# One-core decoder block: a third late MoE unit, x2 added on VectorE, g_final by a transfer, the overflow loop's body written once

## The chip, the cores and the metric

The kernel runs on one core of a Trainium2 chip. The metric is the device time of one launch in microseconds, the median of several runs. TensorE is called PE (its weight loads PEld), VectorE DVE, ScalarE ACT, GpSimd POOL and SyncE SP.

## What is computed

A decoder block on x of 256 tokens by 1024, in float32. A mixer (attention and a gated delta rule) gives x2 = x + mixer. Then comes an expert layer with 32 experts, of which each token takes two, a gate that is computed from the result, and a final norm:

```
def hierarchical_moe(h, ...):                 # gate: top-1 group, top-2 expert
    for e in range(N_EXPERTS):
        hid = jax.nn.silu(t @ w_gate[e]) * (t @ w_up[e])
        out = out + gate[:, e:e + 1] * (hid @ w_down[e])
...
        x = x + hierarchical_moe(rmsnorm(x, g_ffn[i]), ...)
        ple_gate = jax.nn.sigmoid(rmsnorm(x, g_ple[i]) @ w_ple_gate[i])
        x = x + ple_gate * (p[i] @ w_ple_proj[i])
    return rmsnorm(x, g_final)
```

A matrix of one expert (`w_gate`, `w_up` or `w_down`) has 1 MB, `w_ple_gate` 4 MB. x3 is the x behind the expert layer.

## The kernel before

**Units.** The experts are sorted by their load and served in nine units: unit 0 of four experts, units 1 and 2 of two, units 3 to 8 of four. A unit's tokens are gathered by a one-hot matmul into `XT`. Then come `gate(i)` and `up(i)` (64 matmuls of 128x32 weights by 256 columns for a unit of four), `hidden(i)` (the product, its transposes to `hidT`), and the down projection in two halves of 512 columns (`dn`). The weights come as 1-MB matrices into a ring of SBUF buffers (names ra, rq, rb, rc, rs), by indirect transfers that POOL issues in order, each as soon as its buffer is free.

**Early units.** What an early unit computes is spread back to the tokens (`parts`, line 1700): ACT copies the half to `yH`, DVE makes `yL`, the rest, and PE adds both by the one-hot `C` into four PSUM banks `total[t][n]` (tile names `sum00` to `sum11`). x2 itself lies as two parts, `xH` and `xL` (`xx0`, `xx1`), which also feed the gathers. `add_x2` (line 1359) adds it to `total` with eight identity matmuls. After the last early unit `early_features` (line 1899) copies each quarter of `total` to `x3` in the PLE buffer `ple[2]`, and transposes it into the features, a tile that `room` (line 1875) places where `xx0` was.

**Late units.** `UE` is the first late unit, `UL` = 8 the last. Before, units 7 and 8 are late. `z_early` (line 1917) makes the gate's product z = features by `w_ple_gate` from the early part of x3, with 32 float32 matmuls of 512 columns into the four `sum` banks, after `gate(UE)`; it needs `w_ple_gate` in four ring buffers, each scaled by g_ple (`scaled`). The tuple `WPG` says ahead of which unit's which matrices this weight is fetched. A late unit's half goes by `late_parts` and `late_spread` into x3 by DVE adds, its transposed form by `z_late` through the same weight (eight pairs of 64-row matmuls for each half), and by `z_spread` (four matmuls with `C2`, which `rows2` makes) into z. Down weights of units from `UE`-1 on come in halves, so that a first half can start earlier (`FIRST`).

**The overflow branch.** A late expert has 16 or 32 slots; tokens beyond a unit's slots are served by `overflow` (line 1720), a loop over the experts under a condition that is false in this run. The body has four windows of 64 tokens, written out four times (`for win in range(T // 64)`), with 78 matmuls in each. `crowded` (line 1796) puts this branch in, in the middle of unit 4.

**g_final** is read by SP as one row of 4 KB, and spread over the partitions by two matmuls with one row of weights and two ACT copies (`ple_rows`, line 1817).

**Order.** Each piece of work is a generator whose `yield after(...)` names what must have been told. A planner (`Plan`) runs them with a cost model and so fixes the order of instructions on each engine at build time; `turn()` passes the one bank `ga` from user to user. All operations pass through one helper, so that nearly every row of the trace has line 77; tiles tell them apart.

Of the kernel before, what the change touches and what calls it, by code (L numbers as in the profile page):

```python
# [6 lines left out]
F32 = mybir.dt.float32  # L7
# [17 lines left out]
UNITS = [[0, 1, 2, 3], [4, 5], [6, 7]] + [list(range(e, e + 4)) for e in range(8, E, 4)]  # L25
NU = len(UNITS)

WPG = (7, "g")

UE, UL = NU - 2, NU - 1  # L30

FEW = 16
FIRST = UNITS[UE - 1][0]
# [258 lines left out]
def hybrid_block(tc, x, p_t, w_in, w_o_fox, w_o_delta, w_out, w_gate, w_up, w_down, w_ple_gate,  # L292
# [1064 lines left out]
    total = [[None, None], [None, None]]  # L1357

    def add_x2():
        S.copy(identr, ident)  # L1360
        G.memset(late_slots, -1.0)
        G.tensor_copy(late_slots[:, 0:FEW], K("slots")[:, 0:FEW])
        yield after("cb", 4 * 4)
        for t in range(2):
            for n in range(2):
                for part in (xH, xL):
                    P.matmul(total[t][n], identr, part[:, t, :, n * 64:(n + 1) * 64].rearrange("p k q -> p q k"),
                             start=False, stop=False)
                yield
        tell("x2in")  # L1370

    def weights():
# [248 lines left out]
    def rows2(i):  # L1621

        yield after("crowd")
        yield after("rows", i + 1)
        yield after("wt", UE // 2 + 1)
        yield after("lp", 4 * max(0, i - UE - 1))
        yield lambda: None if using else 0.0
        using.append(i)
        g = K("w_rt")[:, 0:256].rearrange("p (t c) -> p t c", t=2)
        for t in range(2):  # L1630
            V.tensor_tensor(g[:, t].rearrange("p (a o s) -> p a o s", a=2, o=4),
                            K("slots")[:, None, None, 0:FEW].to_broadcast([128, 2, 4, FEW]),
                            rkp[:, t, None, UNITS[i][0]:UNITS[i][-1] + 1, None].to_broadcast([128, 2, 4, FEW]), op=OP.is_equal)
        yield
        yield turn()
        pc = ps_t("ga")[:, 0:256]
        for t in range(2):
            P.transpose(pc[:, t * 128:(t + 1) * 128], g[:, t], ident)
        using.pop()
        yield  # L1640

        PR["C2", i] = QD[UE // 2][0].rearrange("p t a s -> p (t a s)")[:, i % 2 * 256:i % 2 * 256 + 256]
        S.copy(PR["C2", i], pc)
        tell("ga")
        tell("C2")
        yield
# [4 lines left out]
    def hidden(i, pg):  # L1651
# [20 lines left out]
        S.copy(hT.rearrange("p k s -> p (k s)"), pt)  # L1672
        tell("hT")
        tell("ga")
        names = [f"d{e}" for e in u]
        yield (ring.there(*names) if u[0] < FIRST else ring.arrived((0, 2), *names))
        w = [ring.get(n).rearrange("p (q k d) -> p q k d", q=4, k=2) for n in names]
# [42 lines left out]
    def overflow():  # L1720
# [12 lines left out]
        with tc.If(n > 0):  # L1733
            V.memset(big[:, 0:1], 1.0)
            V.tensor_copy(rg[:, :, 1:2], gr[:, :, 0, 0:1])
            with tc.For_i(0, E) as e:
# [3 lines left out]
                for i, src in ((0, rko), (2, gr[:, :, :, 1])):  # L1740
                    V.tensor_tensor(prod, src, oh, op=OP.mult)
                    V.tensor_reduce(rg[:, :, i:i + 1], prod, axis=AX.X, op=OP.add)
                for win in range(T // 64):
                    for t in range(2):
                        V.tensor_scalar(g[:, t * 64:(t + 1) * 64], K("slots"), float(64 * win), rg[:, t, 0:1],
                                        op0=OP.add, op1=OP.is_equal)
                    for k in range(8):
                        pt = ps_t("ga")
                        m = 0
# [45 lines left out]

    def crowded():
        yield after("flag")
        yield after("x2in")
        ring.cap -= 2
        yield lambda: ring.free[1][2] if len(ring.free) > 1 else None  # L1800
        yield turn()
        ring.cap += 2
        was = dict(plan.free)
        slots = overflow()
        plan.free.update({key: max(was[k] for k in "PSVG") + 4.0 for key in "PSVG"})
        plan.free["D"], plan.end = was["D"], plan.free["P"]
        for slot in slots:
            ring.give(slot)
        tell("ga")
        tell("crowd")  # L1810
        yield
# [5 lines left out]
    def ple_rows():  # L1817
# [5 lines left out]
            ple.append(ring.take(F32)[0])  # L1823
        pT = ple[1][:, 0:512].rearrange("p (k t) -> p k t", k=2)
        nc.sync.dma_start(pT, p_t.rearrange("(k p) t -> p k t", p=128))
        gf = ple[1][:, 1024:2048]
        nc.sync.dma_start(gf[0:1, :], bass.AP(tensor=g_final.tensor, offset=g_final.offset, ap=[[0, 1], [1, D]]))
        at = plan.load(plan.end, 1 << 18)
        yield after("group", 3)
        yield ring.there("wpp0")  # L1830
# [11 lines left out]
                yield  # L1842
        ring.done("wpp0")
        tell("pp")

        for n in range(2):
            yield turn()
            ps = ps_t("ga")
            P.matmul(ps, ones[0:1, :], gf[0:1, n * 512:(n + 1) * 512], start=True, stop=True)
            yield  # L1850
            S.copy(gf[:, n * 512:(n + 1) * 512], ps)
            tell("ga")
            yield

# [17 lines left out]

    def room():

        yield after("crowd")
        yield after("group", (NU + 1) // 2)
        features.append(mr.tile([128, 2, 8, 128], F32, name="xx0"))
        ring.add(mr, "xx", 1, 2)  # L1880
        yield

    features = []
# [15 lines left out]
    def early_features(t):  # L1899

        yield lambda: 0.0 if len(ple) > 2 and features else None
        for n in range(2):
            yield after(f"done{t}", n + 1)
            x = x3(t)[:, n * 512:(n + 1) * 512]
            (V.tensor_copy if n else S.copy)(x, total[t][n])
            yield
            yield turn()
            pt = ps_t("ga")
            for kk in range(4):
                P.transpose(pt[:, kk * 128:(kk + 1) * 128], x[:, kk * 128:(kk + 1) * 128], ident)  # L1910
            yield
            (S.copy if n else V.tensor_copy)(feat(t)[:, 4 * n:4 * n + 4, :].rearrange("p k q -> p (k q)"), pt)
            tell("ga")
            tell(f"a{t}")
            yield
# [345 lines left out]
```

## Time and profile before

| | |
|---|---|
| median of 3 runs | 523.71 us (522.18 to 524.1) |
| the profiled execution | 521.74 us, its span 519.9 us |
| PE busy | 476.1 us (92%) |
| DVE busy | 223.2 us (43%) |
| ACT busy | 202.3 us (39%) |
| mean granted PE clock | 0.969 |
| moved by DMA | 141.23 MB, mean 272 GB/s |

Of the profiled time 1.84 us lie outside the span. The page gives shares over the whole span, and stages differ: the experts run from about 250 us on, and the branch of `crowded` comes at 336 us. What waits there is read from the waits of PE, the chain of waits that ended last, and the stretches of a few microseconds in which the busy time, the granted clock and the DMA share are given.

### The profile page before, as it was taken

The numbers are of one execution on the slowest core, as the hardware profiler recorded it, in microseconds if no ns is written. First come the engines' busy times: TensorE is split into PE (matmuls) and PEld (weight loads), VectorE is DVE, ScalarE is ACT, GpSimd is POOL, SyncE is SP. The second block draws the span as 40 slices with busy tenths as digits, with TensorE's granted clock in tenths as the row PEclk, the third lists the DMA queues.
The fourth block names the chain that finished last, engine by engine and source line by source line (L and its number), as shares of the span: only waits on it lengthen the run. The fifth ranks groups of instructions, "written<-read, shape, count | busy, mean of one in ns | idle before, by whom it ended". The sixth has DMA issues, their size and how long they took to land. (4 is left out here: it accounts for less than half of the span.)

```text
span 519.9 us, 10333 instructions
## 1 busy us (share of the span) xinstructions
PE 476.1 (92%) x4313; PEld 343.1 (66%) x4313; DVE 223.2 (43%) x532; ACT 202.3 (39%) x465; POOL 127.7 (25%) x153
## 2 busy tenths in 40 slices
PE   7999999999999999998999988867868779989993
PEld 7999998889999999877565544434325444334341
DVE  3888779773646748677232111100011140101146
ACT  5675855657654554424322122121210350100244
POOL 5000461300000000033224443412374363260000
PEclk9999999999999999997999999978989799999998
DMA  8944442222279658986499999999999999960002
GB/s 339 366 166 161 162 167 84 84 83 85 79 296 400 238 200 337 421 319 219 156 422 422 420 421 420 414 418 419 418 348 417 420 412 420 387 242 3 1 0 81
DMA packets 25028, 141.23 MB, mean 272 GB/s; under 512 B 2561, under 2 KB 2833, under 8 KB 11538
## 3 DMA queue, kind: packets, MB, share of 16 engines
q0 software_dynamic: 13744, 82.86, 39.2%
q1 hardware_dynamic: 11090, 57.15, 29.1%
q8 instruction: 35, 0.57, 0.5%
q10 hardware_dynamic: 144, 0.52, 0.3%
q14 instruction: 15, 0.12, 0.1%
HBM read 139.46 MB, written 1.05 MB: 270 GB/s over the span
## 5 line engine op out<-in xcount | busy, mean ns | idle before, releaser
L77 PE MATMUL mm<-hH,ra 128*128 128x256 f32 x624 | 116.4, 285 | 0.0
L77 PEld LDWEIGHTS mm<-hH,ra 128*128 128x128 f32 x624 | 96.1, 189 | 1.5 <-issue 0.3
L77 PE MATMUL mm<-hL,ra 128*128 128x256 f32 x312 | 76.4, 282 | 0.5 <-DVE hL L77 0.5
L77 PEld LDWEIGHTS mm<-hL,ra 128*128 128x128 f32 x312 | 58.8, 189 | 1.4 <-DVE hL L77 0.7
L77 DVE TENSOR_TENSOR ra<-ra,ra 128x1024 fp32r<-128x1024 f32 x39 | 48.1, 1237 | 16.5 <-ACT ra L77 16.4
L77 ACT CAST ra<-ra 128x1024 fp32r<-128x1024 f32 x39 | 40.8, 1053 | 24.0 <-PE mm L77 22.0
L77 PE MATMUL dn<-ra,hidT 128*32 128x512 f32 (+2 forms) x108 | 33.5, 624 | 3.4 <-issue 3.1
L77 POOL CAST xx<-xt 128x1024 fp32r<-128x1024 f32 (+1 forms) x2 | 3.3, 1650 | 126.2 <-ACT td L77 123.6
L77 DVE TENSOR_TENSOR yL<-dn,yH 128x512 fp32r<-128x512 f32 x15 | 10.4, 690 | 53.8 <-ACT yH L77 43.5
L77 PE MATMUL up<-ra,XT 128*32 128x256 f32 (+1 forms) x224 | 30.2, 382 | 0.0
L77 ACT ACTIVATE XT<-ga,kp 128x256 f32<-128x256 f32 (+1 forms) x32 | 12.3, 445 | 38.0 <-PE ga L77 31.8
L77 DVE SCALAR_TENSOR_TENSOR kp<-th,wt,up 128x256 f32<-128x256 f32 x9 | 4.3, 480 | 51.4 <-PE up L77 51.4
L77 PE MATMUL gate<-rq,XT 128*32 128x256 f32 (+1 forms) x176 | 24.6, 383 | 1.7 <-issue 1.6
L77 PE MATMUL up<-rb,XT 128*32 128x256 f32 x144 | 23.9, 381 | 0.5 <-issue 0.3
L77 PE MATMUL gate<-ra,XT 128*32 128x256 f32 (+1 forms) x176 | 24.2, 402 | 0.0
L77 PEld LDWEIGHTS ga<-G,xx 128*128 128x128 f32 x128 | 18.5, 215 | 7.9 <-issue 3.7
L77 PE MATMUL ga<-G,xx 128*128 128x256 f32 (+1 forms) x128 | 20.8, 313 | 2.9 <-ACT XT L77 1.5
L77 ACT CAST yH<-dn 128x512 fp32r<-128x512 f32 x15 | 8.8, 587 | 32.8 <-PE sum L77 19.6
L77 PE MATMUL gate<-rb,XT 128*32 128x256 f32 (+1 forms) x112 | 21.0, 416 | 0.3 <-issue 0.3
L77 PE MATMUL dn<-rb,hidT 128*32 128x512 f32 (+1 forms) x64 | 19.1, 612 | 1.0 <-DVE yL L77 1.0
L77 PEld LDWEIGHTS up<-ra,XT 128*32 128x32 f32 (+1 forms) x224 | 14.7, 115 | 7.7 <-issue 2.3
L77 PE MATMUL dn<-rq,hidT 128*32 128x512 f32 (+1 forms) x40 | 19.5, 753 | 0.3 <-DVE yL L77 0.3
(503 smaller groups left out, 1083.8 us busy)
## 6 DMA issues: line engine op xcount, KB each, us to landing
ra<-in_w_in SPq DMA_DIRECT2D x19, 1024.0 KB, 5.4
ra<-in_w_gate SPq DMA_DIRECT2D x4, 1024.0 KB, 4.8
ra<-in_w_out SPq DMA_DIRECT2D x3, 1024.0 KB
ra<-in_w_down SPq DMA_DIRECT2D x3, 1024.0 KB, 11.3
ra<-in_w_o_fox SPq DMA_DIRECT2D x2, 1024.0 KB, 5.7
rq<-in_w_in SPq DMA_DIRECT2D x2, 1024.0 KB, 11.5
rb<-in_w_up SPq DMA_DIRECT2D x2, 1024.0 KB
rb<-in_w_down SPq DMA_DIRECT2D x2, 1024.0 KB, 15.1
```

Source lines behind the costliest of these rows:

```text
L77: return f(*a, **k)
```

## The change

Five things change.

1. `UE` goes from 7 to 6: units 6, 7 and 8 are late, and x3's early part holds six units, 0 to 5. `WPG` moves with it: the gate weight is fetched ahead of unit 6's gate matrices, and unit 5's down weights come in halves too. `z_early` follows `gate(6)`.
2. `add_x2` makes no matmuls. Two DVE instructions for the two token tiles write xH + xL into `x3`, and `early_features` adds each quarter of `total` to it with a DVE add, where it was a copy by ACT or DVE. `crowded` waits for the fourth early part and no longer for x2.
3. The features lie in a ring buffer that `room` takes once unit 4 is in `total`, and both `xx0` and `xx1` go to the ring once the branch and x2 are through.
4. g_final comes by one transfer with its row read for all 128 partitions (512 KB), issued from ACT's queue in `hidden(8)`. The 4-KB transfer on SP, two matmuls and two ACT copies are gone.
5. The overflow body stands once in a loop (`tc.For_i`), with one more DVE instruction that moves the window on.

```
-WPG = (7, "g")
-
-UE, UL = NU - 2, NU - 1
+WPG = (6, "g")
+
+UE, UL = NU - 3, NU - 1
...
     def add_x2():
...
-        yield after("cb", 4 * 4)
+        yield lambda: 0.0 if len(ple) > 2 else None
         for t in range(2):
-            for n in range(2):
-                for part in (xH, xL):
-                    P.matmul(total[t][n], identr, part[:, t, :, n * 64:(n + 1) * 64].rearrange("p k q -> p q k"),
-                             start=False, stop=False)
-                yield
+            V.tensor_tensor(x3(t).rearrange("p (q k) -> p q k", k=8), xH[:, t].bitcast(F32).rearrange("p k q -> p q k"),
+                            xL[:, t].bitcast(F32).rearrange("p k q -> p q k"), op=OP.add)
+            yield
         tell("x2in")
...
-        yield after("rows", i + 1)
+        yield after("rows", max(i + 1, UE // 2 * 2 + 2))
...
+        if i == UL:
+
+            nc.scalar.dma_start(ple[1][:, 1024:2048], bass.AP(tensor=g_final.tensor, offset=g_final.offset, ap=[[0, 128], [1, D]]))
...
-                for win in range(T // 64):
+                with tc.For_i(0, T // 64):
...
+                    V.tensor_scalar(rg[:, :, 0:1], rg[:, :, 0:1], -64.0, None, op0=OP.add)
...
         yield after("flag")
-        yield after("x2in")
+        yield after("cb", 4 * 4)
         ring.cap -= 2
...
-        gf = ple[1][:, 1024:2048]
-        nc.sync.dma_start(gf[0:1, :], bass.AP(tensor=g_final.tensor, offset=g_final.offset, ap=[[0, 1], [1, D]]))
...
-        for n in range(2):
-            yield turn()
-            ps = ps_t("ga")
-            P.matmul(ps, ones[0:1, :], gf[0:1, n * 512:(n + 1) * 512], start=True, stop=True)
-            yield
-            S.copy(gf[:, n * 512:(n + 1) * 512], ps)
...
     def room():
 
+        yield after("cb", 4 * (UE - 1))
+        ring.cap -= 1
+        yield lambda: ring.free[0][2] if ring.free else None
+        features.append(ring.take(F32)[0].rearrange("p (t k q) -> p t k q", t=2, k=8))
         yield after("crowd")
+        yield after("x2in")
         yield after("group", (NU + 1) // 2)
-        features.append(mr.tile([128, 2, 8, 128], F32, name="xx0"))
-        ring.add(mr, "xx", 1, 2)
+        ring.add(mr, "xx", 0, 2)
...
-            (V.tensor_copy if n else S.copy)(x, total[t][n])
+            V.tensor_tensor(x, x, total[t][n], op=OP.add)
```

How the order moves, at three places. First PE at the overflow branch, in unit 4's gathers. The gather (`G` by `xx`) stands ahead of it, `flag` is the register that the condition reads, and the transposes of `kp` (unit 4's product) come behind. Before:

```order
L77 MATMUL ga_3993<-G_3682,xx1_2737 128x256
L1732 TENSOR_LOAD flag_3191
L1733 COMPARE_AND_BRANCH
L1736 COMPARE_AND_BRANCH
...
L1736 REGISTER_ALU
L1736 COMPARE_AND_BRANCH
L1736 UNCONDITIONAL_BRANCH
L1733 UNCONDITIONAL_BRANCH
L77 MATMUL ga_4567<-kp_67 128x128 x2
```

And now:

```order
L77 MATMUL ga_3986<-G_3682,xx1_2737 128x256
L1734 TENSOR_LOAD flag_3191
L1735 COMPARE_AND_BRANCH
L1738 COMPARE_AND_BRANCH
...
L1745 COMPARE_AND_BRANCH
L1745 UNCONDITIONAL_BRANCH
L1738 REGISTER_ALU
L1738 COMPARE_AND_BRANCH
L1738 UNCONDITIONAL_BRANCH
L1735 UNCONDITIONAL_BRANCH
L77 MATMUL ga_4187<-kp_67 128x128 x2
```

The branch stands at the same place, and what it jumps over went from 312 matmuls to 78, with an inner loop's jumps.

Second PE behind unit 6's gate. Before:

```order
L77 MATMUL gate_4842<-ra7_4620,XT_3177 32x256
L77 MATMUL gate_4842<-ra3_4622,XT_3177 32x256
L77 MATMUL up_4886<-rb2_4706,XT_3177 32x256
L77 MATMUL up_4886<-ra5_4708,XT_3177 32x256
L77 MATMUL up_4886<-ra6_4710,XT_3177 32x256
```

And now, where rq0, rq3 and ra7 hold the gate weight and rb3 the features:

```order
L77 MATMUL gate_4497<-ra6_4330,XT_3177 32x256
L77 MATMUL gate_4497<-rs0_4366,XT_3177 32x256
L77 MATMUL sum00_4540<-rq0_4236,rb3_4336 128x512 x2
L77 MATMUL sum00_4540<-rq3_4238,rb3_4336 128x512 x2
L77 MATMUL sum10_4546<-rq0_4236,rb3_4336 128x512 x2
L77 MATMUL sum10_4546<-rq3_4238,rb3_4336 128x512 x2
L77 MATMUL sum00_4540<-ra7_4240,rb3_4336 128x512
L77 MATMUL up_4552<-ra0_4384,XT_3177 32x256
L77 MATMUL up_4552<-rs1_4386,XT_3177 32x256
```

The first nine matmuls of `z_early` now stand ahead of unit 6's up projection; before, they stood behind unit 7's gate.

Third DVE at unit 5's two down halves (`yL` is the rest of a half, `kp` the product of a unit or the transpose that follows). Before:

```order
L77 TENSOR_TENSOR yL_4799<-dn_4789,yH_4798 128x512
L77 TENSOR_TENSOR yL_4824<-dn_4802,yH_4823 128x512
L77 TENSOR_TENSOR kp_67<-kp_67 128x128 x2
L77 SCALAR_TENSOR_TENSOR th_4883<-th_4883,gate_4842 128x256
L77 SCALAR_TENSOR_TENSOR kp_67<-th_4883,wt_3683,up_4886 128x256
```

And now, where rb4 is x3:

```order
L77 TENSOR_TENSOR yL_4408<-dn_4398,yH_4407 128x512
L77 TENSOR_TENSOR rb4_3885<-rb4_3885,sum00_3512 128x512
L77 TENSOR_TENSOR rb4_3885<-rb4_3885,sum10_3513 128x512
L77 COPY rb3_4336<-ga_4417 128x512
L77 COPY rb3_4336<-ga_4444 128x512
L77 TENSOR_TENSOR yL_4450<-dn_4423,yH_4449 128x512
L77 TENSOR_SCALAR rq0_4236<-rq0_4236,kp_67 128x1024
L77 TENSOR_TENSOR rb4_3885<-rb4_3885,sum01_3553 128x512
L77 TENSOR_TENSOR rb4_3885<-rb4_3885,sum11_3554 128x512
L77 TENSOR_TENSOR kp_67<-kp_67 128x128 x2
```

The early features of the first 512 columns now come between unit 5's two halves, those of the last 512 behind the second, with the scaling of the gate weight among them.

## Rows read from the trace of the kernel before

**Rows 1.** PE's waits, 341 to 512 us: us in total, times, longest us.

```profile
PE ga L77 <- PEq L1733: 4.9, 1, 4.9
PE dn L77 <- issue: 4.5, 3, 2.6
PE gate L77 <- issue: 1.9, 3, 0.8
```

**Rows 2.** Stretches: PE, PEld, DVE, ACT, POOL busy; PE clock, DMA share, GB/s.

```profile
340.00:345.00 5.00, 2.98 (x14) 2.30 (x18) 0.00 (x0) 0.57 (x2) 1.87 (x2) 0.58 1.02 419
435.00:440.00 5.00, 5.00 (x65) 2.53 (x67) 0.00 (x0) 0.00 (x0) 0.00 (x0) 1.00 1.01 421
470.00:475.00 5.00, 5.00 (x13) 2.15 (x12) 0.00 (x0) 0.00 (x0) 0.00 (x0) 1.00 0.01 3
```

**Rows 3.** The chain of waits that ended last: start us, us, what.

```profile
342.69 2.08 PE ga L77 x8
344.77 3.35 PE dn L77 x16
...
374.49 1.05 PE ga L77 x2
...
380.10 1.92 PE dn L77 x16
382.02 2.62 issue
384.64 3.15 PE dn L77 x16
...
392.56 3.59 PE gate L77 x64
...
402.05 1.47 PE ga L77 x12
...
461.98 0.66 PE ga L77 x2
...
468.55 7.06 PE sum L77 x16
...
483.37 1.72 PE gate L77 x8
485.09 1.13 PE sum L77 x4
486.22 1.87 PE gate L77 x8
488.08 1.90 PE dn L77 x16
```

**Rows 4.** Line 1733, the overflow branch, by sequencer: ns min/median/max, start.

```profile
L1733 SPq COMPARE_BRANCH  x1: 45/45/45, 323.4 to 323.4; - x1
L1733 PEldq COMPARE_BRANCH  x1: 6192/6192/6192, 335.0 to 335.0; - x1
L1733 ACTq COMPARE_BRANCH  x1: 45/45/45, 337.2 to 337.2; - x1
```

**Rows 5.** Timeline of ACT at the branch: start us, us, instruction [idle before <-releaser].

```profile
336.66 0.84 ACT L77 ACTIVATE XT<-ga,kp 128x256 f32<-128x256 f32 x2 [7.27 <-PE ga L77]
```

**Rows 6.** Timeline of PE at three places.

```profile
327.49 1.26 PE L77 MATMUL sum<-xx,identr 128*128 128x512 f32 x2
...
328.72 3.17 PE L77 MATMUL sum<-xx,identr 128*128 128x512 f32 x6
...
335.41 1.21 PE L77 MATMUL ga<-G,xx 128*128 128x256 f32 x8
...
417.54 0.66 PE L77 MATMUL ga<-kp,rb 128*128 128x128 f32 x4 [0.21 <-ACT rb L77]
...
424.47 0.44 PE L77 MATMUL ga<-kp 128*128 128x128 f32 x2 [0.68 <-ACT xx L77]
```

**Rows 7.** DVE adds over 1024 columns, from the page's costliest groups.

```profile
L77 DVE TENSOR_TENSOR ra<-ra,ra 128x1024 fp32r<-128x1024 f32 x39 | 48.1, 1237 | 16.5 <-ACT ra L77 16.4
```

More of the change, by code (lines that the diff above doesn't have):

```diff
@@ L1742, in overflow @@
                     V.tensor_reduce(rg[:, :, i:i + 1], prod, axis=AX.X, op=OP.add)
-                for win in range(T // 64):
+                with tc.For_i(0, T // 64):
                     for t in range(2):
-                        V.tensor_scalar(g[:, t * 64:(t + 1) * 64], K("slots"), float(64 * win), rg[:, t, 0:1],
-                                        op0=OP.add, op1=OP.is_equal)
+                        V.tensor_scalar(g[:, t * 64:(t + 1) * 64], K("slots"), rg[:, t, 0:1], None, op0=OP.is_equal)
+                    V.tensor_scalar(rg[:, :, 0:1], rg[:, :, 0:1], -64.0, None, op0=OP.add)
                     for k in range(8):
@@ L1844, in ple_rows @@
         tell("pp")
-        for n in range(2):
-            yield turn()
-            ps = ps_t("ga")
-            P.matmul(ps, ones[0:1, :], gf[0:1, n * 512:(n + 1) * 512], start=True, stop=True)
-            yield
-            S.copy(gf[:, n * 512:(n + 1) * 512], ps)
-            tell("ga")
-            yield
     def scaled():
```

## The prediction

> **What bounds the kernel now.** I read the waits of PE from 341 us on first. Of the 18 kinds of wait listed there none is ended by a transfer; the largest are one of 4.9 us for PE's own sequencer at the overflow branch and three halts of 4.5 us in sum ahead of down projections, for which the profile names no releaser [rows 1]. So in the last third PE waits for itself and for short steps of ACT and DVE, not for weights. The stretches say how far the weights are ahead: the DMA engines are saturated at 340 and at 435 us (share 1.02 and 1.01, 419 and 421 GB/s) and done by 470 (share 0.01) [rows 2]. The weights that come last belong to unit 8's down projection, which starts at 488.08 [rows 3], 18 us later. The chain of waits is then PE's own row of work from 341 to 511 us, with an ACT and DVE tail of some 9 us behind it. What shortens PE's work or its halts there shortens the span one for one, until 18 us of lead are used up. The time of the transfers themselves does not change: the same bytes, less 4 KB, plus 512 KB at the end.
>
> **The change part by part.** The profiled execution took 521.74 us with a span of 519.9; the sum is made against this one, and the result is scaled by 523.71/521.74 to the median.
>
> (a) x2 off PE. The eight identity matmuls stand at 327.49 (1.26 us, two) and 328.72 (3.17 us, six), back to back but for one short matmul, and unit 4's up projection follows at once [rows 6]. From 327.49 to 328.72 + 3.17 = 331.89 are 4.4 us; without the eight PE reaches up some 4.1 us earlier, as the short one stays. The two DVE adds that replace them are of a form not in this trace (a read with a stride); the nearest rows are adds over 1024 columns, 1.24 us each [rows 7]. DVE is busy for 43% of the span, but the pair stands between the `yL` of unit 3's two halves, and what is queued behind it there is a step that PE's additions to `total` wait for. So the gain is between 4.4 and, with both adds waited for, 4.4 − 2.5 = 1.9. I take −4.1, as nothing follows those adds before the end of the early part.
>
> (b) The branch. PE's compare-and-branch at line 1733 took 6.19 us from 335.0 on, where SP's and ACT's took 45 ns each over far shorter jumped code [rows 4]. PE jumped 312 matmuls. A float32 matmul stands in the trace as two matmuls and two weight loads (the row of 16 `sum` matmuls at 468.55 is eight of the program's [rows 3]), an fp32r one as one of each; a window has 30 and 48 of them, so about 120 + 96 = 216 instructions, and the four some 860. It now jumps one window and an inner loop's jumps, some 260. Neither the trace nor a run shows a jump of that length; the bounds are 45 ns, and 6.19 us. I take the short end, because three engines with 40 to 100 rows to jump pay nothing and the price of PE goes with what is far away, but this is the weakest step. What is late next: the transposes behind the branch need the bank `ga`, which ACT frees when its pair of copies ends at 336.66 + 0.84 = 337.50 [rows 5], and the gather ahead of the branch ends at 335.41 + 1.21 = 336.62 [rows 6]. So of the wait of 4.94 some 0.9 stays: −4.0. [...] Without the stall these give −0.9 and −1.4. Sum −6.3, bound 0.
>
> [...]
>
> (c) g_final's two pairs of matmuls cost PE 1.05 us each, one of them at 374.49 [rows 3]: −2.1. The transfer in their place runs when the engines are idle (share 0.01 at 470 us [rows 2]) and is needed only in the final multiplication; it is hidden. Its issue on ACT's queue is a kind that no row here shows; it stands where ACT waits for PE, and were it not hidden I would bound it by a pair of ACT's copies, 0.84 us [rows 5].
>
> (d) Between unit 5's first down half (380.10) and `gate(6)` (392.56) lie 12.5 us [rows 3], with a halt of 2.62 and a second half at half clock (3.15 instead of 1.90). The early features are put in here. At their old place their four steps of add or copy, four transposes and copy go from 417.54 to 424.47, that is 6.9 us, in which PE mostly waits for ACT and DVE [rows 6]. They fill the halt and keep the clock up, which gives back 2.6 + 1.25. Net +3.1; the bounds are +2 (all halts filled) and +5 (nothing given back but part of the clock).
>
> (e) From `gate(6)` to unit 8's down projection there are 488.08 − 392.56 = 95.5 us now. Behind the change PE has this work there, by the rows at full clock [rows 3]: six gate and up projections of 3.59 (21.5), `z_early` four times 7.06 (28.2), four down halves of 1.90 (7.6), four halves of `z_late` of 3.59 (14.4, a half being 1.72 + 1.87), four times z's spread of 1.13 (4.5), eight pairs of the spread to x3 of 0.66 (5.3), 32 gathers of 1.47/12 (3.9), and transposes and weight columns of some 4.5. Sum 89.9. The late work of the third unit is some 10 us of that. What pays for it are gaps: between 400 and 425 us PE now waits for a chain of unit 6's product and of the early features, partly at half clock; `z_early`, 28 us that need only its weight and the features, now stands ready for just these gaps. I leave 4 us of halts without a named releaser, about what two such places cost now [rows 1]. So 93.9 us, −1.6, with the bounds −5.6 (no halts) and +2.5 (8 us of halts).
>
> The order from unit 8's down projection to the end does not change, and the 31.8 us from 488.08 to 519.9 stay.
>
> Sum: −4.1 − 6.3 − 2.1 + 3.1 − 1.6 = −11.0. The profiled time would be 510.7, and 512.7, rounded 513, on the scale of the median. The weights allow it: the lead of 18 us falls to 7.
>
> **The rivals.**
>
> A, the forecast: 513, range 507 to 518 from the bounds of (a), (d) and (e).
>
> B, the branch stalls as before: PE fetches the far side of the jump whether it is 260 or 860 instructions away. Then (b) gives nothing, and the time is 510.7 + 6.3 = 517.0, or 519. For it: that PE's jump is still much longer than the ones that cost 45 ns. Against it: the price itself is 140 times that of the others, so something that depends on the length is at work.
>
> C, slower: the ring starves. The features' buffer is taken out of it while `xx0` is not yet in, and the four buffers of the gate weight are held from unit 6 rather than from unit 7 on, which is five fewer at 1 MB, or 2.5 us of transfer each at 421 GB/s [rows 2], 12.5 us, against a lead that the forecast itself shrinks to 7. Then transfers wait for PE to free buffers and PE for the transfers. A set of four matrices takes 10 us to come, of which the 3.59 us of the projection before it hide a part: 6.4 us for each of the three late units, 19 in all, and 530 to 532. It decides if the DMA share between 385 and 440 us falls below 0.9. Against it: from 341 us on there is no wait for a transfer at all [rows 1], and `xx0` comes to the ring in exchange.
>
> D, the change doesn't do what it says: `z_early` does not fill the gaps, because its weight is scaled or its features are copied too late and PE's order is fixed. Then (e) is some +2.5 and a chain like the old one stays: 517.
>
> **How the numbers follow.** A 0.52, B 0.25, C 0.11, D 0.12. A measurement of this kernel can tell about 0.5% from no change, so faster means under 521.1 and slower over 526.3. A is faster nearly always, B in two of three, D mostly, C never: 0.73 faster, 0.14 same, 0.13 slower. The range of 8 in 10 goes from the low end of A, 507, over B with its own spread of 4 us, to 523.
>
> **What would show it.** (a) no `sum<-xx,identr` on PE, and up(4) some 4 us sooner after gate(4). (b) the duration of PE's compare-and-branch; a granted clock near 1.0 in the 5 us behind it. (c) no one-row matmuls. (d) about 15.5 us from unit 5's first down half to `gate(6)`. (e) about 94 us from `gate(6)` to unit 8's down half, with `sum` matmuls where `issue` halts were; and waits of PE still without a transfer as releaser. A branch of 6 us, a DMA share below 0.9 from 385 to 440 us, or halts of over 8 us in (e) would make it wrong.

## The result, and the profile after

The changed kernel takes 526.83 us (median of 19 runs) where the kernel before takes 523.39 in the same comparison: ratio 1.0052, interval 1.0032 to 1.0072. It is slower by half a per cent; forecast were 513 us. Medians are of all runs; the ratios and their intervals leave out slow runs, those over 1.5% above the fastest of the same kernel (one of the 19 on either side here). The profiled execution took 527.84 us with a span of 525.4, 5.5 us more than before, at the same mean clock of 0.969.

Five places of PE's row of work say where the span went (us from the start of the span; `gate(i)`, `up(i)`, `dn(i)` by their first matmul):

| | before | after | moved | forecast |
|---|---|---|---|---|
| PE goes on behind the branch | 341.56 | 341.06 | -0.5 | -8.1 |
| `gate(5)` | 358.19 | 355.19 | -3.0 | -10.4 |
| `dn(5)` | 380.10 | 373.39 | -6.7 | -12.5 |
| `gate(6)` | 392.56 | 389.10 | -3.5 | -9.4 |
| `dn(8)`, first half | 488.08 | 493.57 | +5.5 | -11.0 |
| end of the span | 519.9 | 525.4 | +5.5 | -11.0 |

Two stretches miss: 7.6 us up to the branch, of which 1.7 come back later, and 10.6 us between `gate(6)` and `dn(8)`. Together they are the 16.5 us between the forecast and the measured span.

**The branch**, which answers to [rows 4]: instruction, ns min/median/max, start.

```profile
L1735 PEldq COMPARE_BRANCH  x1: 353/353/353, 339.0 to 339.0; - x1
```

353 ns and not 6192. The wait that stood first in [rows 1] is down to 1.0 us and ended by ACT. PE's waits of the kernel after from 341 to 520 us: us in total, times, longest.

```profile
PE ga L77 <- ACT rb L77: 11.9, 3, 10.3
PE dn L77 <- issue: 1.7, 2, 1.4
PE ga L77 <- ACT ra L77: 1.4, 2, 0.7
PE sum L77 <- issue: 1.2, 3, 0.8
PE ga L77 <- ACTq L1735: 1.0, 1, 1.0
```

But a new first row is there, with one wait of 10.3 us.

**Ahead of the branch**, the timeline of DVE, then of POOL, then of PE, all of the kernel after: start, us, instruction, idle before and what ended it.

```profile
322.65 4.80 DVE L77 TENSOR_TENSOR rb<-xx,xx 128x1024 f32<-128x1024 f32 x2 [2.10 <-PE dn L77]
327.38 0.67 DVE L77 TENSOR_TENSOR yL<-dn,yH 128x512 fp32r<-128x512 f32 x1
```

```profile
322.79 5.49 POOL L209 DMA_INDIRECT rb<-in_w_gate,idx  x1 [5.34 <-PE dn L77]
332.56 0.94 POOL L209 DMA_INDIRECT ra<-in_w_up,idx  x1 [4.28 <-PE gate L77]
```

```profile
328.10 0.50 PE L77 MATMUL sum<-yL,C 128*128 128x512 f32 x1 [2.15 <-DVE yL L77]
```

The pair that makes x2 takes 4.80 us, 2.40 each, and not 2.5 for both. `yL` of unit 3's second half is queued behind it on DVE, and PE waits 2.15 us for that. The granted clock then falls to 0.50, where it was 1.00 in these 2 us before (columns as in [rows 2]):

```profile
330.00:332.00 2.00, 2.00 (x24) 0.80 (x16) 0.00 (x0) 0.00 (x0) 0.00 (x0) 0.50 1.04 423
```

`gate(4)` takes 8.7 us and not 5.0, the wait of 2.15 us in it. The POOL row is a second effect: the issue of a transfer that begins during the pair lasts until the pair is over, 5.49 us where others take 0.94.

**Between `gate(6)` and `dn(8)`**, the chain of waits of the kernel after (start, us, what), to be held against [rows 3]:

```profile
389.10 6.13 PE gate L77 x64
...
458.00 1.85 PE ga L77 x16
459.85 1.73 PE gate L77 x32
461.58 1.33 PE ga L77 x2
...
463.31 11.13 another core or an unknown queue
474.44 0.02 issue
474.47 0.47 ACT th L77
...
493.57 1.90 PE dn L77 x16
```

and stretches of it, columns as in [rows 2]:

```profile
340.00:345.00 5.00, 3.56 (x25) 1.73 (x25) 0.00 (x0) 2.05 (x5) 3.76 (x4) 1.00 1.02 410
...
390.00:395.00 5.00, 5.00 (x60) 2.25 (x52) 0.00 (x0) 0.56 (x1) 1.04 (x2) 0.58 1.03 410
...
455.00:460.00 5.00, 5.00 (x46) 1.83 (x48) 1.79 (x4) 1.82 (x4) 0.00 (x0) 1.00 0.03 9
460.00:465.00 5.00, 4.41 (x70) 2.30 (x61) 0.00 (x0) 0.93 (x2) 3.78 (x4) 1.00 0.56 187
465.00:470.00 5.00, 0.00 (x0) 0.00 (x0) 0.00 (x0) 0.00 (x0) 3.79 (x4) 0.93 0.75 269
470.00:475.00 5.00, 0.00 (x0) 0.00 (x0) 0.03 (x1) 0.53 (x2) 1.90 (x2) 0.50 0.49 174
```

From 465 to 474 us PE, DVE and ACT do nothing at all; only POOL works, and it issues transfers. ACT waits for unit 8's gate, whose matmuls the profile shows as ended at 463.8 (those ends are modelled); PE waits for ACT. I call this the stop. It is 10.3 us long, and without it the stretch would have taken 104.5 - 10.3 = 94.2 us, forecast 93.9. That the two are so near is in part luck: `gate(6)` takes 6.1 us at a granted clock of 0.58 and not 3.6, while PE's other waits there come to 1.1 us where 4 were allowed.

What runs in the stop is the last of unit 8's down weights. POOL's timeline of the kernel after, and then of the one before:

```profile
446.84 0.94 POOL L209 DMA_INDIRECT rc<-in_w_down,idp  x1 [0.30 <-issue]
460.11 0.94 POOL L209 DMA_INDIRECT xx<-in_w_down,idp  x1 [12.33 <-PE ga L77]
...
471.37 0.95 POOL L209 DMA_INDIRECT xx<-in_w_down,idp  x1 [0.30 <-issue]
```

```profile
444.43 0.94 POOL L209 DMA_INDIRECT ra<-in_w_down,idp  x1 [0.30 <-issue]
453.68 0.94 POOL L209 DMA_INDIRECT rb<-in_w_down,idp  x1 [8.31 <-PE ga L77]
...
465.37 0.95 POOL L209 DMA_INDIRECT xx<-in_w_down,idp  x1 [0.30 <-issue]
```

In both kernels ten transfers are left when POOL has to wait for a buffer, and POOL issues one every 1.25 us. Before, the wait is 8.3 us, and the ten begin 6.4 us ahead of `gate(8)` (460.04). After, the wait is 12.3 us, since the buffer comes free only behind unit 7's second down half; the ten begin 0.4 us behind the start of `gate(8)` (459.67). The DMA engines idle meanwhile (share 0.03), and the last packet lands at 474.29, 0.2 us ahead of the `th` that ends the stop. In the trace of before the same thing can now be seen in a milder form. Its chain of waits in `gate(8)`:

```profile
462.64 1.61 PE gate L77 x19
464.25 0.81 issue
465.06 0.62 PE gate L77 x4
465.69 0.79 issue
```

`gate(8)` took 8.5 us there, twice what it takes without halts, and ended at 468.55; the last packet landed at 468.73.

### The profile page after: what moved, and what is told of

It is laid out like the page before. It is cut to its first block, busy times and chain, and to the rows that moved or that the text cites. A ratio compares the mean times of both kernels' runs of the same rounds, so it can differ in the third digit from the quotient of the medians.

```text
span 525.4 us, 10427 instructions
## 1 busy us (share of the span) xinstructions
PE 478.9 (91%) x4351; PEld 341.8 (65%) x4351; DVE 233.5 (44%) x544; ACT 204.0 (39%) x468; POOL 136.4 (26%) x157
## 5 line engine op out<-in xcount | busy, mean ns | idle before, releaser
L77 PE MATMUL gate<-ra,XT 128*32 128x256 f32 (+1 forms) x208 | 30.6, 419 | 0.0
L77 PE MATMUL gate<-rb,XT 128*32 128x256 f32 (+1 forms) x160 | 25.6, 401 | 0.0
L77 PE MATMUL dn<-ra,hidT 128*32 128x512 f32 (+1 forms) x80 | 24.8, 600 | 0.9 <-ACT hidT L77 0.5
L77 DVE SCALAR_TENSOR_TENSOR th<-th,gate 128x256 f32<-128x256 f32 x9 | 3.8, 420 | 45.3 <-ACT th L77 35.9
L77 PE MATMUL up<-rq,XT 128*32 128x256 f32 x96 | 23.1, 382 | 0.1
L77 PE MATMUL dn<-rq,hidT 128*32 128x512 f32 (+2 forms) x52 | 19.3, 566 | 1.7 <-issue 1.4
L77 PEld LDWEIGHTS ga<-G,xx 128*128 128x128 f32 x128 | 16.2, 189 | 6.9 <-issue 2.9
L77 PE MATMUL ga<-G,xx 128*128 128x256 f32 (+1 forms) x128 | 18.6, 290 | 2.1 <-ACT XT L77 1.6
L77 PE MATMUL up<-rs,XT 128*32 128x256 f32 x96 | 19.1, 382 | 0.1
```

What stands on the lines that cost most here:

```text
L77: return f(*a, **k)
```

## Experiments

**Theories.** T1: the stop belongs to unit 8's late down transfers, it hides the gain, and the third late unit is what made them late. T2: the gain never came, because x2's pair on DVE is too dear or PE's work in (e) larger than counted. T3: the third late unit is simply more work than the gaps it fills. The four runs of the first set fell on a chip on which the kernel before takes 504.93 us; the other sets ran on three chips where it takes 522 to 523. Ratios are always to the kernel before in the same set.

### First set: x2's place, the loop, unit 8's pieces (before 504.93)

`x2_late` puts the pair behind the branch, `x2_pe` puts the eight matmuls back, `unrolled` writes the body four times again, `d8_halves` fetches unit 8's down weights in halves like the other late units'. The changed kernel itself did not run on this chip; `d8_halves`, which differs from it in unit 8's down pieces alone, stands in for it.

```
x2_late:    add_x2():  + yield after("crowd")
x2_pe:      add_x2():  - V.tensor_tensor(x3(t) ..., xH[:, t] ..., xL[:, t] ..., op=OP.add)
                       + P.matmul(total[t][n], identr, part ..., start=False, stop=False)
            early_features():  - V.tensor_tensor(x, x, total[t][n], op=OP.add)
                               + (V.tensor_copy if n else S.copy)(x, total[t][n])
unrolled:   overflow:  - with tc.For_i(0, T // 64):
                       + for win in range(T // 64):
d8_halves:             - return PIECES if u[-1] == E - 1 else HALVES
                       + return HALVES
                       ...
```

> The changed kernel, with the two VectorE adds of x2 placed behind the overflow branch, where VectorE is idle, and no longer between the two halves of unit 3's parts. The trace of the changed kernel has the pair at 322.65, 4.80 us long, with the yL of unit 3's second half behind it, for which PE waits 2.15 us. Theory A: the pair costs what stands behind it, and unit 4's product reaches the branch 3 to 4 us sooner; everything behind shifts with it, so about 523 against the 526.8 of the changed kernel. Rival: PE would have waited for something else there, and the time stays at 527 within 1.

> The changed kernel, with x2 again added by eight identity matmuls into the four sums and with early_features copying the sums to x3, as before; all the rest as changed. Theory A (the VectorE pair delays unit 3's second half by more than the matmuls cost): the matmuls cost 4.3 us on PE again but the wait for yL of 2 us and the late start of what follows are gone: 523 to 524. Rival (the pair is hidden, as was forecast): 4 us slower than the changed kernel, 531.

> The changed kernel, with the overflow body written out four times again. Theory A (the length of the untaken body makes the branch stall): PE's compare-and-branch goes from 0.35 to about 6 us, PE starts again some 5 us later with a lower granted clock behind it, and the whole is 5 to 6 us slower than the changed kernel, 532. Rival (what was won at the branch was not on the path, since unit 8's transfers set the end): no slower, 527.

> The changed kernel, with unit 8's down weights fetched in two halves (8 transfers) and not in one half and two quarters (12); its down projection still runs in three pieces. In the changed kernel PE and ACT stand still from 464 to 474.4 us, while the last ten of these transfers run one behind the other at 1.25 us each, and go on when the last has landed. Theory A (the stop belongs to these transfers): the last lands 4 to 5 us sooner, the stop is that much shorter, and the time is 522. Rival (the stop has another cause and only coincides): it stays, and so does the time, 527.

Measured: x2_late 505.96 (1.0032, 1.0007 to 1.0057), x2_pe 506.15 (1.0031, 1.0009 to 1.0052), unrolled 509.24 (1.011, 1.0068 to 1.0153), d8_halves 506.32 (1.0042, 1.0022 to 1.0063).

The branch of `unrolled`:

```profile
L1735 PEldq COMPARE_BRANCH  x1: 6106/6106/6106, 331.4 to 331.4; - x1
```

The stall is back, and the time with it: 3 us over its neighbours, where 5 to 6 were expected. So step (b) holds: with four windows behind the jump it takes 6.1 us here and 6.2 in the kernel before, with one 0.35 in the kernel after.

None of the four traces has the stop: ACT's `th` of unit 8 stands at 453 to 458 us, 8 to 11 us ahead of the last packet, so `d8_halves` can't answer its question here. In it `dn(8)` follows `gate(6)` by 91.2 us, below the 93.9 forecast. This chip doesn't halt PE there, and still these forms of the change are no faster than the kernel before.

`x2_pe` answers for (a): it comes to `up(4)` at 328.1 us, `d8_halves` with the pair at 327.9, and the times are the same. Here the pair costs just what the eight matmuls cost, where `x2_pe` was expected to be 3 us faster or 4 us slower.

`x2_late` shows where one gain went. Its `gate(4)` takes 5.0 us, with `d8_halves` 8.8, and it is at `gate(5)` 4.3 us sooner (341.8 against 346.1) and at `gate(6)` 4.2 us sooner (375.7 against 379.9); but `gate(6)` ends at 386.0 in the one and at 386.5 in the other. PE's waits of `x2_late` from 370 to 390 us:

```profile
PE gate L77 <- DMA ra<-in_w_gate,idx: 1.4, 1, 1.4
PE gate L77 <- DMA rs<-in_w_gate,idx: 1.4, 1, 1.4
```

Unit 6's gate matrices now come behind the 4 MB of `w_ple_gate` (`WPG`). In `x2_late` PE waits 2.8 us for them, and nearly all that it gained ahead of them is lost. (That they come behind it is from the order of the issues on POOL.) The pair itself keeps its price behind the branch, and holds POOL as before. DVE and POOL of `x2_late`:

```profile
328.82 4.71 DVE L77 TENSOR_TENSOR rb<-xx,xx 128x1024 f32<-128x1024 f32 x2 [0.90 <-DVEq L1736]
```

```profile
330.00 4.35 POOL L209 DMA_INDIRECT rc<-in_w_up,idx  x1 [1.56 <-PE ga L77]
```

### Second set: again, and with two late units (before 521.97)

`after_b` and `before_b` are the two kernels again. `ue7` is the changed kernel with two late units, all else kept. `x2_late_wpg_u` has the pair behind the branch and fetches `w_ple_gate` ahead of unit 6's up matrices.

```
ue7:            - WPG = (6, "g")     + WPG = (7, "g")
                - UE = NU - 3        + UE = NU - 2
x2_late_wpg_u:  - WPG = (6, "g")     + WPG = (6, "u")
                add_x2():  + yield after("crowd")
```

> The kernel before, unchanged, for its trace on the chip on which the next three run. In the last call the kernel before took 504.9 us and not 523, and none of four traces had a stop of PE and ACT as at 464 us in the first trace of the changed kernel. Theory A (what differs between the two chips is stretches in which PE's work takes longer than its instructions say): its trace has no halts of PE without a releaser ahead of down projections and in unit 8's gate, and these 10 us and more are the difference. Rival: all PE work is shorter by the same share.

> The changed kernel, unchanged. Theory A (the stop of 10.6 us belongs to the other chip, as do halts of a like sum in the kernel before, so that it does not make the difference): no stop here and the same ratio to the kernel before, 1.003 to 1.006. Rival (the stop makes the changed kernel slower): without the stop it is 8 to 10 us faster than the kernel before, ratio 0.98.

> The changed kernel with two late units again (UE = 7, the gate weight ahead of unit 7's gate); x2 on VectorE, the features in a ring buffer, the transfer of g_final and the loop stay. Theory A (a third late unit gives nothing, since its late work of some 10 us on PE only takes the place of halts): within 0.3% of the changed kernel. Rival 1 (the third late unit is what costs): 3 to 6 us faster than the changed kernel, and faster than the kernel before. Rival 2 (it gives what was forecast): 2 us slower or more.

> The changed kernel with the x2 adds behind the overflow branch (x2_late) and with the gate weight fetched behind unit 6's gate weights, ahead of its up weights. In the trace of x2_late PE comes to unit 6's gate 4 us sooner, but that gate takes 10.3 us and not 6, as two of its four weights, which come behind the 4 MB of the gate weight, land during it. Theory A (that wait ate what x2_late won): no wait for a transfer in gate(6), and 3 to 4 us less than x2_late, ratio to the kernel before 0.995. Rival (the gate weight, now 10 us later, is waited for by z_early instead): no better than x2_late, 1.003.

Measured: before_b 521.5, after_b 526.11 (1.0069, 1.0047 to 1.0091), ue7 516.79 (0.9896, 0.9868 to 0.9924), x2_late_wpg_u 519.14 (0.9932, 0.9908 to 0.9957).

The stop of `after_b`, in its chain of waits:

```profile
460.19 11.00 another core or an unknown queue
471.19 0.02 issue
471.22 0.47 ACT th L77
```

It comes again, 10.3 us without work on PE, and ends when the last packet has landed (471.20). So the stop belongs not to one chip alone, and neither theory of `after_b`, both of which went by a chip without it, was put to the test. With two late units the other edits gain 1%, with three the whole costs 0.7%: 9.3 us between two kernels of one set. In `ue7` POOL's wait is 8.3 us, and the ten transfers begin 6.4 us ahead of `gate(8)` (450.24 and 456.60), both as in the kernel before; its `gate(8)` takes 8.5 us, as there. So the third late unit is what made them late (rival 1 of `ue7`, by more than it said). `x2_late_wpg_u` has the three late units, no wait for a transfer in `gate(6)` (383.0 to 386.7, 3.7 us) and no long stop, and gains 0.7%, as its theory A said; but `dn(8)` follows 98.4 us later and not 93.9, with halts in many places.

### Third set: the stop itself (before 522.2)

`d8_cut` doesn't issue the second halves of unit 8's down weights, and its down projection uses the first half twice (so eight of the last transfers are left out, and what they bring). `d8_halves_b` is `d8_halves` on a chip with the stop. `x2_late_ue7` has two late units and the pair behind the branch. `before_c` is the kernel before.

```
d8_cut:  - self.rows(t[:, a:b], src, self.pieces[j][...])
         + if not (j[0] and name in [f"d{e}" for e in UNITS[-1]]):
         +     self.rows(t[:, a:b], src, self.pieces[j][...])
         ...
         - w[o][:, a:b, k, :]
         + w[o][:, a % 2:a % 2 + b - a, k, :]
```

> The kernel before, unchanged, for its trace beside the next three. On a chip on which it takes about 522 us, as twice now: the halts of the first trace at the same places (4.9 us at the branch, 2.6 ahead of unit 5's second down half, 8.5 us for unit 8's gate). On one on which it takes about 505: the 4.9 us at the branch alone, from unit 6's gate to unit 8's down projection about 85 us and not 95.

> The changed kernel without the eight transfers of the second half of unit 8's down weights; the pieces of its down projection take the columns of the first half in their place, so that part of the result is left out. In both traces of the changed kernel with the stop, PE stands still in unit 8's gate until within 0.3 us of the landing of the last of these transfers; the gate of the kernel before (8.5 us and not 4.2) ends there too. Theory A (PE is held up as long as these transfers run): on a chip with the stop, unit 8's gate ends within 1 us of the landing of the first halves, 8 to 10 us sooner than in the changed kernel, and the time falls by as much, 517. Rival (it is held up by something at this place of the program): the stop stays, 526.

> The changed kernel with unit 8's down weights in two halves and not in three pieces, again: the first time it ran on a chip without the stop and took 1.0042 times the kernel before. Theory A (the stop lasts as long as the transfers): on a chip with the stop these end some 5 us sooner, and the time is 521 to 522 where the changed kernel takes 526. Rival: 526. On a chip without the stop: 506, as the first time.

> The changed kernel with two late units again and with the x2 adds behind the overflow branch: what the other parts of the change are worth. Two late units alone (ue7) were 9.3 us faster than the changed kernel and 5.2 faster than the kernel before. Theory A (the VectorE pair of 4.8 us delays unit 4 by 3 to 4 us, and nothing later hides that): 3 us less than ue7, ratio to the kernel before 0.983 to 0.985. Rival (a later wait takes it up, as in x2_late): 0.989 as ue7.

Measured: before_c 521.69, d8_cut 512.14, d8_halves_b 519.1 (0.9934, 0.9907 to 0.9962), x2_late_ue7 514.63 (0.984, 0.9785 to 0.9895).

The chain of waits of `d8_cut` in unit 8's gate, and one of its stretches:

```profile
456.55 1.73 PE gate L77 x32
458.27 0.37 PE ga L77 x2
458.64 1.86 PE gate L77 x32
460.51 0.60 PE ga L77 x4
```

```profile
460.00:465.00 5.00, 4.54 (x32) 1.74 (x24) 1.11 (x2) 1.22 (x3) 0.00 (x0) 1.00 0.32 109
```

With the eight transfers gone, `gate(8)` takes 4.2 us, nothing halts, and the whole is at 512.14. That is one run, 5 us below the 517 that were expected of it; it moves 2 MB less and leaves part of the result out, so that it is near the 513 of the forecast says little. `d8_halves_b` moves all the bytes, but has four transfers fewer, with the last four twice as large; its stop in the chain of waits:

```profile
460.46 5.42 another core or an unknown queue
465.88 0.02 issue
465.90 0.47 ACT th L77
```

PE is held for 4.6 us and not 10.3, and the kernel is 0.7% faster than the one before. So the stop hangs on these transfers, and on their number more than on their bytes; T1 holds for the size of it. But here it ends 4.5 us ahead of the last packet (470.42): it isn't a plain wait for the last landing. `x2_late_ue7` is where its theory A put it.

### Fourth set: the loop alone, and the transfers' order (before 522.62)

`before_loop` is the kernel before with the loop's body written once and nothing else. `d8_first` fetches unit 8's down weights ahead of its up matrices. `late3_best` is this with the pair behind the branch, `ue7_best` the same with two late units.

```
before_loop:  - for win in range(T // 64):
              + with tc.For_i(0, T // 64):
d8_first:     + if i == UL:
              +     ups = [r for r in q[n:] if r[0][0] == "u"]
              +     q[n:] = [r for r in q[n:] if r[0][0] != "u"] + ups
```

> The kernel before with one part of the change: the overflow body stands once in a loop. Theory A (the forecast's step for the branch): PE's compare-and-branch takes 0.4 us, the time is 6 us shorter, ratio 0.988. Rival (part of it is given back, as in the changed kernel, where the second up half ahead of the branch got slower and gate(6) came 6.6 us earlier and not 9.4): 2 to 4 us, ratio 0.993 to 0.996.

> The changed kernel with unit 8's down weights fetched ahead of its up weights: the twelve small transfers go out as soon as unit 7's gate weights are used, and two up matrices of 1 MB take the buffers for which unit 8's down weights waited. Theory A (the small transfers hold up PE, in unit 8's gate): on a chip with the stop, it shrinks from 10.5 to at most 2 us, and the time is 517 to 518, ratio 0.990. Rival (any transfer that POOL issues at that place holds it up): a stop of 3 to 5 us, 521. On a chip without the stop: no change, 1.004.

> The changed kernel, three late units, with the x2 adds behind the branch and unit 8's down weights ahead of its up weights. Theory A (the third late unit's work of some 10 us on PE is worth what it fills once nothing else is late): gate(6) waits some 3 us for its weights behind the gate weight, else as the forecast: 513 to 515, ratio 0.982 to 0.985. Rival (the third late unit costs more than it fills in any case): slower than ue7_best by 3 us or more.

> As late3_best with two late units (UE = 7, the gate weight ahead of unit 7's gate weights). x2_late_ue7 had a ratio of 0.984 with unit 8's gate still taking 8.5 us and not 4.2. Theory A: that shrinks by 3 to 4 us, ratio 0.976 to 0.978. Rival (with two late units the stop in unit 8's gate is only other work that is slower there): 0.984.

Measured: before_loop 517.74 (0.9904, 0.9864 to 0.9944), d8_first 520.87 (0.9972, 0.996 to 0.9985), late3_best 518.57 (0.9915, 0.9897 to 0.9932), ue7_best 514.54 (0.9827, 0.9789 to 0.9865).

The branch of `before_loop`, in the code of the kernel before:

```profile
L1733 PEldq COMPARE_BRANCH  x1: 358/358/358, 335.2 to 335.2; - x1
```

This one edit brings 4.9 of the 6.3 us that were forecast for it, between its theory and its rival; its ten runs lie between 514.1 and 520.7. At `gate(6)` it is even 8.4 us ahead (384.1, against the first trace of the kernel before), and `dn(8)` then follows after 98.7 us and not 95.5: a part is given back to halts. Its `gate(8)` takes 8.5 us as before. The chain of waits of `d8_first`:

```profile
448.82 8.35 another core or an unknown queue
457.17 0.02 issue
457.19 0.59 ACT yH L77
...
462.80 1.73 PE gate L77 x32
464.53 0.37 PE ga L77 x2
464.90 1.86 PE gate L77 x32
```

`gate(8)` runs free in 4.2 us, but a halt of 3.9 us of PE has come ahead of it, behind unit 7's second half, again without a named releaser. The order of the last transfers moves the stop and makes it smaller; it doesn't take it away, which is what the rival of `d8_first` said. With the same order and the same place of x2, two late units (`ue7_best`) are 4 us faster than three (`late3_best`), as the rival of `late3_best` said. That speaks for T3 beside T1, but doesn't isolate it: `gate(6)` takes 6.2 us in `late3_best` behind the early features (in the kernel after 6.1, at a granted clock of 0.58), and 3.7 in both kernels with x2 behind the branch and two late units. These two, `x2_late_ue7` and `ue7_best`, are 1.6 and 1.7% faster than the kernel before. The order of the transfers adds nothing there that shows, as the rival of `ue7_best` said.

**What stays open.** Why PE stands while POOL issues these transfers. The stop is no dependence that the program has: the same form of the kernel runs through on the chip of the first set, and there ACT's `th` of unit 8 comes 8 us ahead of the last packet. On the other chips it ended within 0.4 us of the last packet in eight of the traces (`before` three times, `after` twice, `before_loop`, `ue7`, `x2_late_ue7`), and in the others it didn't. What the five longest stops (3.8 to 10.3 us of idle PE) share is POOL's unbroken series of issues: the signal of PE that the next engine waits for comes 1.5 to 2.3 us behind its end, wherever the last packet stands. In the kernel before a late signal comes 1.6 us behind (467.93, series until 466.32).

| | POOL's series ends | PE's signal comes | last packet of POOL's queue lands |
|---|---|---|---|
| `after` | 472.32 | 474.44 | 474.29 |
| `after_b` | 469.20 | 471.19 | 471.20 |
| `d8_halves_b` | 464.43 | 465.88 | 470.42 |
| `d8_first` | 454.89 | 457.17 | 471.57 |
| `late3_best` | 453.21 | 455.46 | 470.97 |

In the kernel after, the signals of the gate's last matmul and of the four transposes behind it come 0.06 us apart (474.44 and 474.50), though these four take 0.6 us by their rows. So it looks as if PE's work was done and the telling of it came late; as matmul ends are modelled, that is argued and not shown. Smaller delays of PE's signals (0.7 to 2.8 us in the kernel after) stand beside POOL's other issues in all 14 traces from chips with the stop, those of the kernel before among them; the four traces of the first set have none of over 0.5 us but at the long branch of `unrolled`. Nor are instructions missing by the trace: the instruction queues moved nothing from 457 to 484 us in the kernel after. The kernel before has no trace from the chip of the first set, so why it is no slower there than the changed forms isn't shown either.

## Why the prediction was wrong

**(a), x2 off PE: wrong, by 7.6 us.** Forecast were -4.1 up to the branch; PE came 3.5 us later (339.0 and not 335.5, where `up(4)` ends). The step that failed is the bound of the DVE pair from contiguous adds [rows 7]: 2.4 us each and not 1.24, with the strided reads. (That the stride alone doubles it isn't shown: POOL's issue always ran beside the pair.) With 4.8 us in place of 2.5 my own far end, 4.4 minus the pair, would have read a loss of 0.4. I also saw what is queued behind the pair, "a step that PE's additions to `total` wait for", and then took -4.1 "as nothing follows those adds before the end of the early part"; the two don't go together, and that step was the path: `gate(4)` is 3.7 us longer, 2.15 of it idle and the rest at the lower clock (0.84, 0.50 and 0.80 in the stretches of 2 us from 328 on), and 1.0 us was lost ahead of it. The sign given for (a), `up(4)` some 4 us sooner after `gate(4)`, did come (0.5 us behind its end and not 4.3), but the price had been paid ahead of it. In `after_b` `gate(4)` took 7.3 us, and PE was 0.5 us later than in `before_b` and not 3.5; so some 3 of the 7.6 us differ from one pair of traces to the other. Moving the pair behind the branch restores `gate(4)`. A rest of 2.4 us, `up(4)` with 6.1 us in place of 3.7 through halts without a releaser, comes in all traces with x2 off PE on the chips with the stop (also in `x2_late_wpg_u`, where the pair stands later), and not on the chip of the first set. With x2 off PE, `up(4)` runs while POOL issues a series of four transfers (332.56 to 337.23 in the kernel after); before, x2's matmuls stood beside that series (327.82 to 332.49). It is the pattern of the stop on a small scale, and no run isolates it.

A second price of the pair was not in the sum at all: it holds POOL's issue of transfers. In all 13 traces with the pair the last issue that overlaps it ends 0.8 us behind the pair, wherever the pair stands. It cost no bandwidth here: the DMA share stayed at 1.00 and more, and by the bytes that POOL's queue had moved the transfers then ran 12 us and more behind their issue (an estimate; in the kernel after 31 transfers of 1 MB, 32.5 MB, had been issued by 322.79 us and 26.8 MB moved, and the 5.7 MB between them are 13.7 us at the 418 GB/s of the stretch to 328.28; in the chain of waits of `x2_late` the transfer that was held stands for 19.48 us, from 330.00). Why the pair holds the issue no run shows.

**(b), the branch: right.** 353 ns, 1.0 us of wait left (forecast 0.9), a granted clock of 1.00 from 340 to 345 us where it was 0.58. Rival B is out. `before_loop` gives -4.9 us of the whole, `unrolled` takes 3 us back.

The wait is -4.0 of the sum of (b). Its -0.9 and -1.4, for the eight gathers and unit 4's first down half behind the branch, no run shows as such. What the runs show: the gathers took 2.08 us before, at a granted clock of 0.50, and 1.20 in the kernel after, at 1.00; the half took 3.35 before, at 0.57, and 3.17 after, at 1.00, with a halt of 0.30 in it; in `before_loop` they take 2.06 and 2.83, at 0.79 from 340 to 345 us. From the branch to `gate(5)` the kernel after gains 2.5 us.

These runs show that the length of the body decides, 6.1 and 6.2 us at some 860 instructions and 0.35 to 0.36 at some 260 (both counted in the forecast), and not at which size the price comes.

**(c), g_final, and (d), the early features: right, the first with luck.** From `gate(5)` to `dn(5)` 18.2 us and not 21.9 (-3.7, forecast -2.1). The 1.6 beyond the forecast are not g_final: the first half of `gate(5)` took 3.4 us before, at a granted clock of 0.54, and 1.9 now, at 1.00. From `dn(5)` to `gate(6)` 15.7 us and not 12.5 (+3.25, forecast +3.1). So `gate(6)` came 3.5 us earlier where 9.4 were forecast, and the difference is (a), less these 1.6. But (d) has a price that was not in its sum: ahead of `gate(6)` PE is busy for 2.7 of 5 us (385 to 390), and `gate(6)` runs at 0.58 and takes 2.5 us more, which stand in (e).

**(e), from `gate(6)` to `dn(8)`: the sum of PE's work right, the allowance for halts wrong.** 104.5 us, of which 10.3 are the stop; 94.2 without it, and 91.6 in `d8_cut`. The list of 89.9 us was for full clock; `gate(6)`'s 2.5 us took the room of halts that didn't come. The step that failed is "I leave 4 us of halts without a named releaser": I took halts that I could not explain as a constant that moves with nothing, and in the kernel before they stood just in `gate(8)`, beside the transfers for unit 8's down half. I had also written that "the lead of 18 us falls to 7", and asked of it only whether the weights still come in time. They did; what decided was that they were issued during `gate(8)` and not ahead of it. The prediction's own sign for this, halts of over 8 us in (e), came. Rival D is out: `z_early` does fill the gaps, and 94.2 us is its price. Rival C was near with its mechanism, transfers that wait for PE to free buffers (POOL's wait of 12.3 us), but it looked between 385 and 440 us, where the DMA share stayed at 0.91 or more, and the starved stretch is at 455 (0.03).

**And the size of the whole.** No pair of runs shows a gain by the third late unit. The list in (e) puts its work at ten us of PE; the gaps that this fills seem to be worth no more. `ue7` against `after_b`, 9.3 us, has the stop in it; `ue7_best` against `late3_best`, 4 us, has a smaller one on either side. On the chip without a stop the kernels with three late units are 0.3 to 0.4% slower than the one before (1.1% unrolled), but none with two ran there, so what the unit itself costs isn't isolated.

**The tail** kept its 31.8 us, with the transfer of g_final in it.

## What to carry to other kernels

Price a VectorE instruction from a row with the same access pattern; where there is none, try the sum with twice the contiguous row (here it was 1.9 times, 2.40 us against 1.24) before you say which way the edit goes, and look at what stands behind it on its queue and which engine waits for that. When work is moved to a later unit, follow the buffers that this unit frees, to the last transfers and to what PE does when they are issued. A halt without a releaser isn't a constant to carry over: see which transfers are issued beside it, and what the change does to their place. A long body that is jumped over was worth writing once here, 4.9 us of 522.6.

## What the runs showed of the hardware

- The jump of PE over the overflow body took 6.0 to 6.2 us over four unrolled windows (the kernel before and `unrolled`) and 0.35 us over one (the kernel after, `before_loop` and others).
- An add of 1024 columns in float32 with strided reads took 2.3 to 2.4 us on DVE (half the pair), a contiguous one 1.24.
- While that pair ran, an indirect transfer's issue on POOL took up to 5.49 us and not 0.94, and ended 0.8 us behind the pair.
- PE, ACT and DVE stood for up to 10.3 us while ten transfers of 256 and 512 KB were issued 1.25 us apart, on the chips where the kernel before takes 522 to 523 us and not on the one where it takes 504.93. The signal of PE that ended the five longest stops came 1.5 to 2.3 us behind POOL's last issue.
